# The matmuls for a norm's factors placed behind a stage's first products, in a two-layer model of mixers, attention and experts in fp32

## The chip, the cores and the metric

One core of a Trainium2 chip runs the whole program as one launch. The metric is the device time of an execution in microseconds. Runs of the kernel before agree within 0.1%, so a difference of more than 0.2% is one that its measurement can tell.

## The reference

256 tokens of width 1024 (`h`) go through two layers of a first kind and two of a second kind, all in fp32. Every stage starts with an RMS norm and ends in an addition to `h`:

```python
def rmsnorm(x, g):
    y = x * rsqrt(mean(x * x, axis=-1, keepdims=True) + EPS) * g

# first kind, layers 0 and 1
h = mixer_block(h, ...)            # norm; h @ w_in; retention and gated delta rule; merged @ w_out
u = rmsnorm(h, norm_ffn)
h = h + swiglu(u, ...)             # layer 0: dense, d_ff 2816
h = h + moe(u, ...)                # layer 1: 8 experts of 1408, the best 2 of each token
h = h + sigmoid(rmsnorm(h, norm_ple) @ w_ple_gate) * (p @ w_ple)
# then h = rmsnorm(h, norm_final), and the second kind, layers 0 and 1
u = rmsnorm(h, norm1_g_2)
proj = u @ w_in_2                  # heads of three mixers: attention, an mLSTM, an HGRN
h = h + concat(attention, mlstm, hgrn) @ w_out_2
u = rmsnorm(h, norm2_g_2)
h = h + relu(u @ w_up_2) ** 2 @ w_down_2
```

## The kernel before

`h` lies transposed in SBUF as `hT` (128 channels by 8 blocks `k` by 256 tokens). TensorE runs each fp32 product as three passes: every activation and every weight is split into a rounded part and the remainder (`uhi`, `ulo`, `whi`, `wlo`), and hi·hi, hi·lo and lo·hi are added in PSUM. A product of the stage's input with one weight piece of 256 columns is 48 matmuls of 128x256 (8 blocks, 2 halves, 3 passes).

`piece` (its lines 219, 230 and 231) brings one weight piece of 1 MB in on SyncE's queue, and splits it in two halves: ScalarE rounds (`whi`), VectorE subtracts (`wlo`). `whi` and `wlo` have four half buffers each, so two pieces are split at a time, and the raw pieces have two buffers (in the experts' stage four, `wraw` and `xraw`). Whoever calls `piece` with a pool loads a piece `ahead`, without splitting it.

`norm_T` (L421) makes the stage's input: ScalarE scales `hT` by the norm's gain (`uhi`, L430), VectorE makes `ulo` (L431), both squared on the way into a sum over the 8 blocks (`t`, L402 to L410). The norm's factor per token is left out of `u`; the products are scaled by it afterwards. `by_token` (L418) sums `t` over channels with two matmuls of one column, `rsqrt` (L340 to L351) is a chain of 13 small VectorE operations on 128x2, and `along_tokens` (L444) lays the factor along the free axis: VectorE makes a diagonal `dg` (L453), a matmul of `ones` with it gives `pr` (L454), and ScalarE copies it out as `rsT` (L455). `norm_twice` does it for two norms in a row.

The stages that matter below are `ffn` (layer 0), `moe` (layer 1), `ple`, `_second` (the mixers of the second kind) and `ffn2`. `_second` runs its parts in the order of the list `SECOND`: `hqf` (the first product, in `gemm_b` with `wave`), `mvo`, attention's `aq`, `ak`, `av`, steps of a scan `s`, four steps of attention `a` (each: scores `sm<-ak,aq`, maxima on VectorE, exponentials `pp` on ScalarE, `aa` on VectorE, transposes `sm<-c_base,aa`, a copy `at` on ScalarE, and `sm<-av,at`), `mqk` (the mLSTM's q and k, L1519), `hig`, and the mLSTM's steps `m`. In `mqk` the product in PSUM is multiplied by `rsT` (`cx`, L1527), goes through a convolution of width 4 along the tokens on ScalarE and VectorE (L1532 and L1534), a sigmoid (L1350 to L1352), and becomes `mq` and `mk` (L1538), which the mLSTM multiplies on TensorE (`sm<-mq,mk`, L1731).

`moe` ends with `values_load(mosti)` and `tc.If(n > 128)`: every engine loads the largest number of tokens that an expert has, compares, and takes the branch for a second pass over the experts only where it is above 128 (with these inputs it isn't).

The engines run their own queues in order. What order that is is decided when the program is built: a scheduler of the tile framework orders each engine's instructions by the program's order and by its own estimate of when operands and buffers are free.

Of the kernel before, what the change touches and what calls it, by code (L numbers as in the profile page):

```python
# [150 lines left out]
class Kernel:  # L151
# [102 lines left out]
    def gemm_b(self, x, w, c0, cb, width=256, n=2, tt=False, wave=False):  # L254

        ps = [self.bank("acc") for _ in range(2)]
        if wave:
            wts = [self.piece(w, 0, c0 + i * width) for i in range(n)]
            for t in range(2):
                for j in range(8):  # L260
                    for i in range(n):
                        self.gemm_tok(x, [p[j:j + 1] for p in wts[i]], ps[t][:, i * width:(i + 1) * width], t, k0=j,
                                      start=i == 0 and j == 0, stop=i == n - 1 and j == 7)
                cb(t, ps[t])
            return
# [155 lines left out]
    def norm_T(self, name, rs, xs=None):  # L421
# [18 lines left out]
        r = self.rsqrt(self.by_token(s), 2)  # L440
        rs += [r[:, t:t + 1] for t in range(2)]
        return u
# [15 lines left out]
    def norm_twice(self, n0, n1, rs):  # L458
# [14 lines left out]
        r0 = self.rsqrt(self.by_token(s0), 2)  # L473
        m1 = self.sm.tile([128, 2], F32, name="m01", bufs=1)
        nc.vector.tensor_tensor(m1, r0, r0, OP.mult)
        nc.vector.tensor_tensor(m1, m1, self.by_token(s1), OP.mult)
        r1 = self.rsqrt(m1, 2, name="rt")
        r01 = self.sm.tile([128, 2], F32, name="r01", bufs=1)
        nc.vector.tensor_tensor(r01, r0, r1, OP.mult)
        rs += [r01[:, t:t + 1] for t in range(2)]  # L480
        rT = self.along_tokens([r0[:, t:t + 1] for t in range(2)], name="r0T")
        for k in range(8):
            h = self.hT[:, k, :]
            nc.vector.scalar_tensor_tensor(h, h, g0[:, k:k + 1], rT, op0=OP.mult, op1=OP.mult)
        return u
# [13 lines left out]
    def _mixer(self, l):  # L499
# [5 lines left out]
        if l:  # L505
            rs = []
            u = self.norm_T("norm_mix.1", rs)
            r2 = one([128, 2], "r2")
            rh = [r2[:, t:t + 1] for t in range(2)]
        else:  # L510
            u = self.norm_t(self.rows["norm_mix.0"])
            rs, rh = [1.0] * 2, [0.5] * 2
        convw, gr, gdngn = one([128, 24, 4], "convw"), one([128, 16], "gr"), one([128, 1], "gdngn")
# [114 lines left out]
        def ret_v(i):  # L628
            def cb(t, ps):
                nc.scalar.activation(rv[:, t, i * 512:(i + 1) * 512], ps, AF.Copy, scale=rs[t])  # L630
            self.gemm_b(u, W, 1024 + i * 512, cb, wave=i == 0 and l == 1)
# [194 lines left out]
    def ple(self, l, ple):  # L826
        nc = self.nc
        rs = []
        u = self.norm_T(f"norm_ple.{l}", rs)
        half = self.sm.tile([128, 2], F32, name="half", bufs=1)  # L830
        for t in range(2):
            nc.vector.tensor_scalar(half[:, t:t + 1], rs[t], 0.5, None, op0=OP.mult)
        rT = None
        for i in range(4):
            ps = self.bank("acc")
            self.gemm_a(u, self.piece(f"w_ple_gate.{l}", 0, i * 256), ps, wave=i == 0)
            if rT is None:
                rT = self.along_tokens([half[:, t:t + 1] for t in range(2)])
            two = lambda x: x.rearrange("p (n t) -> p n t", n=2)
            g = self.t2("pg")  # L840
            h = self.hT[:, 2 * i:2 * i + 2, :]
            nc.vector.tensor_tensor(two(g), two(ps), rT[:, None, :].to_broadcast([128, 2, T]), OP.mult)
# [4 lines left out]
    def ffn(self):  # L847
        nc = self.nc
        with self.tc.tile_pool(name="pl0", bufs=1) as self.pp, self.tc.tile_pool(name="ffn", bufs=2) as self.mp:
            rs = []  # L850
            ple, parts = self.ple_table(0)
            u = self.norm_T("norm_ffn.0", rs)
# [4 lines left out]
            down = None  # L857
            for i in range(11):
                ps = []
                for w in ("ffn_w_gate", "ffn_w_up"):  # L860
                    wt = self.piece(w, 0, i * 256)
# [18 lines left out]
                if i < 10:  # L880
                    down = lambda i=i, x=x: self.down_T(x, self.piece("ffn_w_down", 2 * i, 0), acc, i == 0, False)
            self.last_down_T(x, self.piece("ffn_w_down", 20, 0), acc, scale=rsT)
# [1074 lines left out]
```

## Time and profile before

| | us |
|---|---|
| time, median of 3 runs (2192.87 to 2193.52) | 2193.49 |
| the profiled execution, its own time | 2195.91 |
| its span, first to last instruction | 2194.1 |
| TensorE busy in the span | 2066.0 |
| VectorE busy | 1554.9 |
| ScalarE busy | 1212.1 |
| mean granted TensorE clock | 0.963 of full speed |

TensorE has work in 94% of the span; it is idle for 128 us, 10 of them at the start. The granted clock takes two values, full (2.4 GHz) and half (1.2 GHz), and a matmul that runs at half takes about twice as long, while it still counts as busy. So a wait of TensorE may cost more than its own length.

### The profile page before, as it was taken

How to read it: one execution, taken by the hardware profiler on the slowest of the kernel's cores; microseconds unless marked ns; L12 is line 12 of the kernel's file. 1: busy time of each engine (PE TensorE's matmuls, PEld its weight loads, DVE VectorE, ACT ScalarE, POOL GpSimd, SP SyncE). 2: the span in 40 equal slices, each digit the busy share in tenths (PEclk: the TensorE clock that was granted, in tenths of full speed). 3: DMA queues.
4: the chain of work that ended last, by engine and by line, in shares of the span. 5: the costliest groups of instructions: out<-in, count | busy, mean ns of one | idle time of the engine just before them, and what ended most of it. 6: DMA issues, size and time to landing. Idle time of an engine off the chain costs nothing. (4 is left out here: it accounts for less than half of the span.)

```text
span 2194.1 us, 38904 instructions
## 1 busy us (share of the span) xinstructions
PE 2066.0 (94%) x15686; PEld 1977.4 (90%) x15686; DVE 1554.9 (71%) x2837; ACT 1212.1 (55%) x1798; POOL 38.5 (2%) x89
## 2 busy tenths in 40 slices
PE   7999999999899999999999999789789998978999
PEld 7999998999799999988898898788689998878998
DVE  5889486555877986778888888777664557766444
ACT  5554445444564554467777777564445555544554
POOL 0000000000000000000000000020000002000000
PEclk9999999999999999999999999899699999979999
DMA  5454444555445452658989899342135554213553
GB/s 212 164 183 164 126 139 155 193 192 182 142 159 170 173 164 97 223 191 309 330 312 338 302 336 343 123 153 99 56 116 184 185 190 155 97 59 120 188 185 142
DMA packets 81260, 403.03 MB, mean 184 GB/s; under 512 B 25232, under 2 KB 25393, under 8 KB 45361
## 3 DMA queue, kind: packets, MB, share of 16 engines
q1 hardware_dynamic: 61056, 391.66, 50.3%
q10 hardware_dynamic: 17888, 4.39, 1.0%
q0 software_dynamic: 2128, 4.43, 0.7%
q8 instruction: 124, 2.03, 0.4%
q14 instruction: 64, 0.52, 0.1%
HBM read 398.35 MB, written 2.10 MB: 183 GB/s over the span
## 5 line engine op out<-in xcount | busy, mean ns | idle before, releaser
L231 DVE TENSOR_TENSOR wlo<-wraw,whi 128x1024 fp32r<-128x1024 f32 (+3 forms) x644 | 735.6, 1156 | 389.8 <-ACT whi L230 380.4
L230 ACT ACTIVATE whi<-wraw 128x1024 fp32r<-128x1024 f32 (+3 forms) x644 | 634.3, 1005 | 592.2 <-PE acc L251 192.8
L251 PE MATMUL acc<-whi,uhi 128*128 128x256 f32 (+3 forms) x1920 | 554.0, 299 | 22.0 <-DVE hx L1426 12.8
L251 PE MATMUL acc<-whi,ulo 128*128 128x256 f32 (+3 forms) x1920 | 552.5, 298 | 3.8 <-DVE ulo L431 3.8
L251 PE MATMUL acc<-wlo,uhi 128*128 128x256 f32 (+3 forms) x1920 | 546.6, 299 | 8.0 <-DVE wlo L231 7.4
L251 PEld LDWEIGHTS acc<-whi,uhi 128*128 128x128 f32 x1920 | 361.5, 193 | 27.9 <-issue 13.2
L251 PEld LDWEIGHTS acc<-wlo,uhi 128*128 128x128 f32 x1920 | 359.2, 193 | 15.5 <-DVE wlo L231 14.6
L251 PEld LDWEIGHTS acc<-whi,ulo 128*128 128x128 f32 x1920 | 362.0, 193 | 5.0 <-DVE ulo L431 4.2
L293 PE MATMUL sm<-uhi,whi 128*128 128x256 f32 x864 | 244.3, 283 | 0.0
L293 PE MATMUL sm<-ulo,whi 128*128 128x256 f32 x864 | 243.6, 282 | 0.0
L293 PE MATMUL sm<-uhi,wlo 128*128 128x256 f32 x864 | 243.5, 282 | 0.0
L293 PE MATMUL acc<-uhi,whi 128*128 128x256 f32 x704 | 199.3, 284 | 10.2 <-ACT whi L230 10.2
L293 PE MATMUL acc<-uhi,wlo 128*128 128x256 f32 x704 | 199.6, 284 | 1.7 <-DVE wlo L231 1.7
L293 PE MATMUL acc<-ulo,whi 128*128 128x256 f32 x704 | 199.3, 284 | 1.3 <-DVE ulo L317 1.3
L231 DVE TENSOR_TENSOR wlo<-xraw,whi 128x704 fp32r<-128x704 f32 (+1 forms) x176 | 166.0, 978 | 34.1 <-ACT whi L230 31.5
L230 ACT ACTIVATE whi<-xraw 128x704 fp32r<-128x704 f32 (+1 forms) x176 | 144.4, 860 | 50.6 <-PE acc L251 15.6
L293 PEld LDWEIGHTS sm<-uhi,whi 128*128 128x128 f32 x864 | 165.6, 192 | 0.6
L293 PEld LDWEIGHTS sm<-ulo,whi 128*128 128x128 f32 x864 | 165.0, 191 | 0.6
L293 PEld LDWEIGHTS sm<-uhi,wlo 128*128 128x128 f32 x864 | 164.9, 191 | 0.0
L293 PEld LDWEIGHTS acc<-uhi,whi 128*128 128x128 f32 x704 | 134.0, 191 | 10.8 <-ACT whi L230 10.4
L293 PEld LDWEIGHTS acc<-uhi,wlo 128*128 128x128 f32 x704 | 134.0, 190 | 2.2 <-DVE wlo L231 2.1
L293 PEld LDWEIGHTS acc<-ulo,whi 128*128 128x128 f32 x704 | 133.9, 190 | 1.9 <-DVE ulo L317 1.7
(650 smaller groups left out, 3355.9 us busy)
## 6 DMA issues: line engine op xcount, KB each, us to landing
wraw<-in_w_in SPq DMA_DIRECT2D x80, 1024.0 KB, 4.8
wraw<-in_w_up SPq DMA_DIRECT2D x32, 1024.0 KB, 4.8
wraw<-in_w_down SPq DMA_DIRECT2D x32, 1024.0 KB, 4.8
xraw<-in_exp_w_down SPq DMA_DIRECT2D x24, 1024.0 KB, 7.3
xraw<-in_exp_w_gate SPq DMA_DIRECT2D x32, 704.0 KB, 5.3
xraw<-in_exp_w_up SPq DMA_DIRECT2D x32, 704.0 KB, 5.6
wraw<-in_exp_w_gate SPq DMA_DIRECT2D x32, 704.0 KB, 5.4
wraw<-in_exp_w_up SPq DMA_DIRECT2D x32, 704.0 KB, 5.8
```

The source lines that it names most:

```text
L230: nc.scalar.activation(hi[:, :mm], raw[:, s], AF.Copy)
L231: nc.vector.tensor_tensor(lo[:, :mm], raw[:, s], hi[:, :mm], OP.subtract)
L251: nc.tensor.matmul(o, a[:, k0 + j, ts], b[j], start=start and i == 0 and j == 0, stop=stop and i == 2 and j == n - 1)
L293: self.nc.tensor.matmul(ps[:, n * 256:(n + 1) * 256], a[j][:, n * 128:(n + 1) * 128], b[:, j, :], start=(n, j, i) == (0, 0, 0), stop=(n, j ...
```

## The change

Nothing is computed otherwise. In text order:

- `norm_T` and `norm_twice` return the input and a function `fin`, which holds `by_token`, the rsqrt chain (and in `norm_twice` the scaling of `hT`). The caller runs `fin`, and `along_tokens` behind it, after the stage's first products.
- The first weight piece of a stage is asked for ahead of `norm_T`, so that its split stands ahead of the norm's tiles on ScalarE and VectorE.
- `gemm_b` with `wave` goes over blocks 0 to 5 for both token halves and then over 6 and 7, and calls `mid` (there `fin`) ahead of its callbacks.
- In `_second`, `rsT` is made in this `mid`, and no longer in `mqk`.
- `ple` makes two of its four products ahead of `fin`.
- The last step of `ffn` and of the first `ffn2` makes its up products ahead of the previous step's down products.
- `moe` runs the branch ahead of the main pass over the experts, and loads one experts' piece `ahead` instead of one of `w_ple_gate.1`.

```diff
     def gemm_b(self, x, w, c0, cb, width=256, n=2, tt=False, wave=None, mid=None):
         ps = [self.bank("acc") for _ in range(2)]
         if wave:
-            wts = [self.piece(w, 0, c0 + i * width) for i in range(n)]
+            for js in (range(6), range(6, 8)):
+                for t in range(2):
+                    for j in js:
+                        for i in range(n):
+                            self.gemm_tok(x, [p[j:j + 1] for p in wave[i]], ps[t][:, i * width:(i + 1) * width], t, k0=j,
+                                          start=i == 0 and j == 0, stop=i == n - 1 and j == 7)
+            mid()
             for t in range(2):
-                for j in range(8):
...
                 cb(t, ps[t])
             return
...
     def norm_T(self, name, rs, xs=None):
...
-        r = self.rsqrt(self.by_token(s), 2)
-        rs += [r[:, t:t + 1] for t in range(2)]
-        return u
+        def fin():
+            r = self.rsqrt(self.by_token(s), 2)
+            rs.extend(r[:, t:t + 1] for t in range(2))
+
+        return u, fin
...
     def ple(self, l, ple):
...
+        wt = w(0)
+        u, fin = self.norm_T(f"norm_ple.{l}", rs)
...
+        self.gemm_a(u, wt, ps[0], wave=True)
+        self.gemm_a(u, w(1), ps[1])
+        fin()
...
+        rT = self.along_tokens([half[:, t:t + 1] for t in range(2)])
...
     # ffn
-            u = self.norm_T("norm_ffn.0", rs)
+            first = self.piece("ffn_w_gate", 0, 0)
+            u, fin = self.norm_T("norm_ffn.0", rs)
             for f in parts:
                 f()
...
                     self.gemm_a(u, wt, ps[-1], wave=i == 0 and len(ps) == 1)
-                    if rsT is None:
-                        rsT = self.along_tokens(rs)
...
+                if i == 0:
+                    fin()
+                    rsT = self.along_tokens(rs)
...
     # moe
-        self.experts(uk, pos, ghl, rhl, 0)
...
-        self.piece("w_ple_gate.1", 0, 0, self.pp)
+        self.piece("exp_w_gate.0", 0, 0, self.pp)
         n = nc.values_load(mosti[0:1, 0:1], min_val=0, max_val=256)
+        ahead, self.ahead = self.ahead, {}
         with self.tc.If(n > 128):
             self.experts(uk, pos, ghl, rhl, 1)
+        self.ahead = ahead
+        self.experts(uk, pos, ghl, rhl, 0)
...
     # _second
+        wave = [self.piece(W, 0, 2568 + i * 256) for i in range(2)]
...
-            self.gemm_b(u, W, 2568, cb, wave=True)
+            def mid():
+                fin()
+                rsT.append(self.along_tokens(rs))
+
+            self.gemm_b(u, W, 2568, cb, wave=wave, mid=mid)
...
         def g_mqk():
-            rsT.append(self.along_tokens(rs))
             for i, nm in enumerate(("q", "k")):
...
     # ffn2
+            first = self.piece(f"w_up_2.{l}", 0, 0)
+            u, fin = self.norm_T(f"norm2_g_2.{l}", rs)
...
-                if i == 3 and not l:
-                    rsT = self.along_tokens(rs2)
...
+                if i == 3:
+                    fin()
+                    for t in range(2):
+                        nc.vector.tensor_tensor(rs2[t], rs[t], rs[t], OP.mult)
+                    if not l:
+                        rsT = self.along_tokens(rs2)
```

How the built programs stand, at three places. First TensorE's queue in the mixers of layer 0, where the last steps of attention (`av`, `at`, `aa`), the factor's matmuls (`dg`) and the last products of `hig` meet the first of the mLSTM; before:

```order
L1809 MATMUL sm<-av,at 128x128
L1810 MATMUL sm<-av,at 128x128
L1811 MATMUL sm<-av,at 128x128
L454 MATMUL sm<-dg,ones 128x128 x2
L251 MATMUL acc<-wlo,uhi 128x256
L251 MATMUL acc<-whi,uhi 128x256
L251 MATMUL acc<-whi,ulo 128x256
L251 MATMUL acc<-wlo,uhi 128x256
L1731 MATMUL sm<-mq,mk 128x256
L1732 MATMUL sm<-mq,mk 128x128
L1805 MATMUL sm<-c_base,aa 128x128 x3
L1809 MATMUL sm<-av,at 128x128
```

The same place of the changed kernel:

```order
L1836 MATMUL sm<-av,at 128x128
L1837 MATMUL sm<-av,at 128x128
L1838 MATMUL sm<-av,at 128x128
L1758 MATMUL sm<-mq,mk 128x256
L1759 MATMUL sm<-mq,mk 128x128
L251 MATMUL acc<-wlo,uhi 128x256
L251 MATMUL acc<-whi,uhi 128x256
L251 MATMUL acc<-whi,ulo 128x256
L251 MATMUL acc<-wlo,uhi 128x256
L1832 MATMUL sm<-c_base,aa 128x128 x3
```

The factor's two matmuls are gone from here (they stand some 580 rows ahead, among the first products), and the mLSTM's first scores stand ahead of the last four products.

Second VectorE's queue at the end of the same stage, around the mLSTM's k (`mk`) and attention's last step (maxima `amx` and `anb`, weights `aw` and `aa`); the changed kernel:

```order
L1700 COPY_PREDICATED hS<-c_second,sm 128x128x2
L1813 TENSOR_REDUCE amx<-sm 128x3
L1565 TENSOR_TENSOR mk<-cv,sg 128x512
L1814 TENSOR_TENSOR amx<-amx 128x1
L1813 TENSOR_REDUCE amx<-sm 128x3
L1816 SCALAR_TENSOR_TENSOR anb<-amx,ars 128x2
L1814 TENSOR_TENSOR amx<-amx 128x1
L1816 SCALAR_TENSOR_TENSOR anb<-amx,ars 128x2
L1574 TENSOR_SCALAR hx<-acc,r_20855 128x256
L1823 RECIPROCAL aw<-osum 128x4
L1824 COPY oss<-aw 128x2
```

`mk` stands inside attention's last step, and the convolutions that it needs stand ahead of that; in the kernel before `cx`, both convolutions and `mk` stand behind the whole step.

Third TensorE's queue in `ffn` of layer 0, behind the 96 matmuls of the first gate and up products; the changed kernel:

```order
L296 MATMUL sm<-uhi,wlo 128x256
L421 MATMUL sm<-ones,t_4178 128x1 x2
L460 MATMUL sm<-dg,ones 128x128
L296 MATMUL sm<-uhi,whi 128x256
L296 MATMUL sm<-ulo,whi 128x256
```

`by_token`'s two matmuls (`ones,t`) now stand right ahead of the diagonal's (`dg,ones`), which needs the rsqrt chain between them; before, 96 rows stood between the two.

## Rows read from the trace of the kernel before

**Rows 1.** The page: busy us by engine, and DMA busy by slice.

```profile
PE 2066.0 (94%) x15686; PEld 1977.4 (90%) x15686; DVE 1554.9 (71%) x2837; ACT 1212.1 (55%) x1798; POOL 38.5 (2%) x89
...
DMA  5454444555445452658989899342135554213553
```

**Rows 2.** TensorE's timeline (start, duration, instruction, idle before and its releaser).

```profile
1551.01 0.61 PE L454 MATMUL sm<-dg,ones 128*128 128x128 f32 x4
...
1566.06 1.19 PE L1731 MATMUL sm<-mq,mk 64*128 64x256 f32 x2 [13.97 <-DVE mk L1538]
...
1592.11 0.77 PE L768 MATMUL acc<-uhi,whi 128*128 128x256 f32 x2
```

**Rows 3.** The timeline of VectorE, the first operation on `mqk`'s products.

```profile
1552.07 0.69 DVE L1527 TENSOR_TENSOR cx<-acc,rsT 128x512 f32<-128x512 f32 x1 [0.22 <-ACT rsT L455]
```

**Rows 4.** The timeline of TensorE, the last of the 96 products of `mqk`.

```profile
1530.69 0.28 PE L293 MATMUL acc<-uhi,wlo 128*128 128x256 f32 x1
```

**Rows 5.** Windows: us, busy of PE, PEld, DVE, ACT, POOL; clock, DMA share, GB/s.

```profile
1500.00:1505.00 5.00, 5.00 (x20) 3.69 (x19) 1.53 (x7) 1.98 (x5) 0.00 (x0) 0.50 0.01 3
1522.00:1528.00 6.00, 6.00 (x56) 5.01 (x55) 4.34 (x14) 0.23 (x2) 0.00 (x0) 1.00 0.00 0
1566.00:1592.10 26.10, 25.46 (x113) 22.94 (x114) 14.78 (x55) 6.16 (x14) 0.00 (x0) 0.50 0.00 1
1955.00:1967.00 12.00, 11.26 (x60) 10.31 (x60) 10.86 (x47) 3.68 (x8) 0.00 (x0) 0.52 0.00 1
1631.00:1638.30 7.30, 7.30 (x64) 7.30 (x64) 3.31 (x4) 3.88 (x6) 0.00 (x0) 1.00 0.30 93
```

**Rows 6.** The timeline of TensorE at the same place of layer 1.

```profile
1942.44 0.28 PE L251 MATMUL acc<-wlo,uhi 128*128 128x256 f32 x1
1954.90 1.23 PE L1731 MATMUL sm<-mq,mk 64*128 64x256 f32 x4 [12.18 <-DVE mk L1538]
```

**Rows 7.** The timeline of ScalarE, then (last row) of VectorE.

```profile
1547.46 0.49 ACT L1807 ACTIVATE at<-sm 128x384 f32<-128x384 f32 x1
1549.53 1.06 ACT L230 ACTIVATE whi<-wraw 128x1024 fp32r<-128x1024 f32 x1 [0.88 <-PE acc L251]
...
1571.10 1.15 ACT L1822 ACTIVATE sq<-mix 128x512 f32<-128x512 f32 x2
...
1578.27 1.29 DVE L1830 TENSOR_TENSOR mix<-mix,or 128x512 f32<-128x512 f32 x2
```

**Rows 8.** The timeline of TensorE at the start of both `ffn2`.

```profile
1624.72 0.56 PE L418 MATMUL sm<-ones,t 128*128 128x1 f32 x2 [7.89 <-DVE t L410]
...
1638.20 0.28 PE L293 MATMUL sm<-uhi,wlo 128*128 128x256 f32 x1
...
2004.02 0.98 PE L418 MATMUL sm<-ones,t 128*128 128x1 f32 x4 [7.87 <-DVE t L410]
...
2018.92 0.28 PE L293 MATMUL sm<-uhi,wlo 128*128 128x256 f32 x1
```

**Rows 9.** The timeline of TensorE in `ffn`, then of VectorE in `ffn2`.

```profile
359.89 1.01 PE L418 MATMUL sm<-ones,t 128*128 128x1 f32 x4 [4.57 <-DVE t L410]
...
2005.04 0.16 DVE L340 TENSOR_SCALAR rq<-sm 128x2 f32<-128x2 f32 x1 [1.17 <-PE sm L418]
...
2007.41 0.23 DVE L1841 TENSOR_TENSOR rs<-rq 128x1 f32<-128x1 f32 x2
```

**Rows 10.** The branch (L988, ns min/median/max); the page's DMA issues; ScalarE's timeline.

```profile
L988 PEldq COMPARE_BRANCH  x1: 3646/3646/3646, 1386.3 to 1386.3; - x1
...
xraw<-in_exp_w_gate SPq DMA_DIRECT2D x32, 704.0 KB, 5.3
...
1391.31 0.63 ACT L402 ACTIVATE t<-hT 128x512 f32<-128x512 f32 x1 [7.30 <-DVEq L988]
```

**Rows 11.** TensorE's timeline in `ple` and `_second`, both of layer 1.

```profile
1397.17 0.58 PE L293 MATMUL acc<-uhi,whi 128*128 128x256 f32 x1 [10.22 <-ACT whi L230]
...
1835.88 0.56 PE L251 MATMUL acc<-whi,uhi 128*128 128x260 f32 x1 [5.34 <-DVE hx L1426]
```

More of the change, by code (lines that the diff above doesn't have):

```diff
@@ L252, in gemm_tok, with gemm_b @@
                                  stop=stop and i == 2 and j == n - 1)
[L254 removed]
+    def gemm_b(self, x, w, c0, cb, width=256, n=2, tt=False, wave=None, mid=None):
         ps = [self.bank("acc") for _ in range(2)]
         if wave:
[L258 removed]
+            for js in (range(6), range(6, 8)):
[5 more added lines that the diff above has]
+            mid()
             for t in range(2):
[L260 to L263 removed]
                 cb(t, ps[t])
@@ L472, in norm_twice, with fin @@
             step1(p)
[L473 to L485, printed above, removed]
+        def fin():
+            r0 = self.rsqrt(self.by_token(s0), 2)
+            m1 = self.sm.tile([128, 2], F32, name="m01", bufs=1)
+            nc.vector.tensor_tensor(m1, r0, r0, OP.mult)
+            nc.vector.tensor_tensor(m1, m1, self.by_token(s1), OP.mult)
+            r1 = self.rsqrt(m1, 2, name="rt")
+            r01 = self.sm.tile([128, 2], F32, name="r01", bufs=1)
+            nc.vector.tensor_tensor(r01, r0, r1, OP.mult)
+            rs.extend(r01[:, t:t + 1] for t in range(2))
+            rT = self.along_tokens([r0[:, t:t + 1] for t in range(2)], name="r0T")
+            for k in range(8):
+                h = self.hT[:, k, :]
+                nc.vector.scalar_tensor_tensor(h, h, g0[:, k:k + 1], rT, op0=OP.mult, op1=OP.mult)
+        return u, fin
     def mixer(self, l):
@@ L506, in _mixer @@
             rs = []
-            u = self.norm_T("norm_mix.1", rs)
+            wave = [self.piece(W, 0, 1024 + i * 256) for i in range(2)]
+            u, fin = self.norm_T("norm_mix.1", rs)
             r2 = one([128, 2], "r2")
@@ L630, in cb @@
                 nc.scalar.activation(rv[:, t, i * 512:(i + 1) * 512], ps, AF.Copy, scale=rs[t])
-            self.gemm_b(u, W, 1024 + i * 512, cb, wave=i == 0 and l == 1)
+            self.gemm_b(u, W, 1024 + i * 512, cb, wave=wave if i == 0 else None, mid=fin)
         def ret(h):
@@ L856, in ffn @@
             acc = [self.bank("acc") for _ in range(4)]
-            down = None
+            down, last = None, []
             for i in range(11):
@@ L881, in ffn @@
                     down = lambda i=i, x=x: self.down_T(x, self.piece("ffn_w_down", 2 * i, 0), acc, i == 0, False)
+                    if i == 9:
+                        last, down = [down], None
+            last[0]()
             self.last_down_T(x, self.piece("ffn_w_down", 20, 0), acc, scale=rsT)
@@ L927, in _moe @@
         nc.vector.tensor_copy(lT, pl[0:8, :T])
+        parts[2]()
+        fin()
         for t in range(2):
@@ L1879, in ffn2 @@
                     down = lambda i=i, x=x: self.down_T(x, self.piece(f"w_down_2.{l}", 2 * i, 0), acc, i == 0, False)
+                    if i == 14:
+                        last, down = [down], None
             if l:
@@ L1885, in ffn2 @@
             else:
+                last[0]()
                 self.last_down_T(x, self.piece(f"w_down_2.{l}", 30, 0), acc, scale=rsT)
```

36 lines of the change are left out of this document (16 added, 20 removed).

## The prediction, made before the run

> **What bounds the kernel now.** I read the page first: TensorE is busy in 94% of the span, VectorE in 71%, ScalarE in 55% [rows 1]. So time is won where TensorE waits, and where it works at half clock. I then listed every TensorE row with idle time in front of it (the timeline), and set windows around them for the granted clock. The idle rows are few and long, and they have two causes. Five stand where a stage begins: the sum of squares `t`, or what is computed from it, or a weight split is last [rows 8, 9, 11]. The two longest stand inside the mixers of the second kind, and their releaser is `mk`, the mLSTM's k [rows 2, 6]. The reader should see in the windows what follows a long wait: from 1566 to 1592 us TensorE has matmuls all the time, at a clock of 0.50 [rows 5]. Such a stretch counts as busy and costs twice its work.
>
> **The long waits for `mk`.** The 96 products that `mk` and `mq` come from are done at 1530.7 us [rows 4], but the first operation on them, `cx`, starts at 1552.07 and waited last for ScalarE's `rsT` [rows 3]. The two matmuls that `rsT` comes from ran at 1551.01 [rows 2], because `mqk` asks for them in text order behind most of attention. So the whole chain of two convolutions and two sigmoids, 1552.07 to 1566, lies behind the last work that could have covered it. The change makes `rsT` in `mid`, some 580 rows of TensorE earlier. The changed order shows what the scheduler makes of it: `cx` and the convolutions now stand between attention's steps, and `mk` stands inside the last step.
>
> *Term D, layer 0.* Removed: the idle 13.97 us [rows 2]. What comes in its place: ScalarE's `at` now stands behind a split `whi` whose buffer becomes free with the last products, and a copy: 1.06 + 0.49 + 0.49 us (the copy taken like `at`) [rows 7], of which TensorE's three transposes cover half a us, so 1.5 us of new wait. The convolutions' VectorE work, now between attention's maxima and weights, delays its steps: not in the trace, bounded by 0 and 3, taken as 1.5. If the clock stays at half in the tail all the same, D is 13.97 - 1.5 - 1.5 = 11.0. If it stays full, the 25.46 us of work at 0.50 [rows 5] shrink by 12.7, but then attention's own chain becomes late: from its squares to its scaled result takes 1571.10 to 1579.56 [rows 7], and TensorE, twice as fast, is there some 2.5 us ahead. D is then 11.0 + 12.7 - 2.5 = 21.2. Which of the two? A stretch of small matmuls without idle stands at full clock from 1522 to 1528, another at half from 1500 to 1505 [rows 5]; so both occur, and I take the middle, **16**.
>
> The Trainium skill (TensorE: Matmul & The Clock Gate, "HAM oscillation — how this bites in real kernels") puts the fall of the clock down to idle gaps. By that rule the tail would run at full clock and D would be 21.2; the stretch from 1500 to 1505 is TensorE at half with no idle, so the trace does not bear the rule out alone.
>
> *Term G, layer 1.* The same place: idle 12.18 [rows 6], and 11.26 us of work at 0.52 [rows 5]. Half clock kept: 12.18 - 1.5 - 1 = 9.7. Full: + 5.6 - 2 = 13.3. Taken **11.5**.
>
> **The starts of both `ffn2`.** Now TensorE waits until `t` is summed, does `by_token`, and only then the first up product; from the last product of the stage before (1624.72 - 7.89 = 1616.83) to the end of the first two up products (1638.48) are 21.65 us; in layer 1 from 1996.15 to 2019.20, 23.05 us [rows 8]. The 96 matmuls of two products need 0.114 us each at full clock (7.30 us for 64 [rows 5]), so 10.9. In the changed order the first piece's split stands ahead of the norm's tiles, `by_token` stands some 250 rows later, and its chain and diagonal are well apart there, so nothing waits for them. What is left is that the blocks of `u` arrive one pair after another. If that costs nothing, the stages win 21.65 - 10.9 = 10.7 and 23.05 - 10.9 = 12.1. If it keeps the clock at half through one of the two products, 5.5 less: 5.2 and 6.6. Middles: *term E* **8** and *term H* **9.3**.
>
> **The start of `ffn`.** *Term A.* The idle 4.57 [rows 9] in front goes. But `by_token` and `dg` are now neighbours on TensorE, and the rsqrt chain must run between them: 1.17 us to its first operation, 2.6 to its end (2005.04 to 2007.64 [rows 9]), and the diagonal behind it. So about 4.3 us of wait come back some 15 us later, with the same drop of the clock. Bounds +2.8 (the clock doesn't drop at one of the two) and -2.9 (it drops at both); I take **-1**. Behind them on TensorE's queue are the third gate and up products, which have nothing else to wait for.
>
> **`ple` and the mixers of layer 1 of the first kind.** *Term B.* The edits there replace short waits by short waits (VectorE has the second piece's split ahead of three of four `ulo` pairs). Bounds 0 and -2.8, one clock drop; taken **-1**.
>
> **The experts.** *Term C.* The branch is moved, not removed. At the end of the experts it holds ScalarE for 7.30 us [rows 10], and TensorE sits idle 10.22 us [rows 11]. There it goes, and TensorE can win up to 8. But `norm_twice` behind `ple` needs `ple`'s result, and its factor is now made behind two products instead of one: most of it is waited for again, and I keep 2.2. At the front, every engine now reads the register and fetches behind the branch: 3.65 us on TensorE [rows 10], in front of the gather. And SyncE, which in the order before asks for five pieces of weights ahead of the register's load, now asks for all but one behind the branch: 5.3 us until one lands [rows 10] and some 2 to split it, against about 5 of gather and first piece. Together -6 (-4 to -9). C is **-3.8**, bounds -9 and +4.
>
> The Trainium skill prices a compare-and-branch at about 108 ns (Advanced Engine Details and Errata, "Control Flow Timing"), and says elsewhere that a branch breaks the sequential prefetch (Runtime: NRT & Kernel Launch, "Instruction fetch mechanics"). By the first alone the entry would cost 2.4 instead of 6 and C would be -0.2; the trace's 3646 ns on TensorE's queue speaks for the second.
>
> **The start of the mixers in layer 1 of the second kind.** *Term F.* The idle 5.34 [rows 11] has the releaser `hx`, which stands behind two weight splits on VectorE. That order is unchanged, and two diagonals now stand ahead of `hx`: **-0.7**, bounds -1.5 and +0.5.
>
> **The sum.** -1 - 1 - 3.8 + 16 + 8 - 0.7 + 11.5 + 9.3 = 38.3 us. The profiled execution would go from 2195.9 to 2157.6, and the median of the runs, which is 2.4 below it, to **2155**. All lower bounds together give a gain of 16 (2177), all upper ones of 65 (2129).
>
> **Rivals.**
> 1. *The tail keeps half clock and attention pays for the convolutions.* TensorE does not wait for `mk` any more, but for `aa` and `at`, whose VectorE and ScalarE work now queues behind `cv` operations; the order speaks for it (six of them stand inside one step), the trace's idle VectorE there against it. D and G at their lower bounds less 3 us each, entry at -9: 38.3 - 8 - 4.8 - 5.2 = 20; time 2173.
> 2. *The clock holds through both tails.* D 21.2, G 13.3, E and H at their upper bounds: 38.3 + 5.2 + 1.8 + 2.7 + 2.8 = 51; time 2143.
> 3. *The change doesn't do what it says:* the `mk` wait is replaced by an equally long one, since the mLSTM's steps also need attention's last step out of the way. Then D and G fall to about nothing, and 11 are left: 2183. If the starts of `ffn2` give nothing either, it is the same as before.
> 4. *Slower: the experts' weights are late throughout.* The experts' stage runs 176 pieces (8 experts of 22) with DMA busy nine tenths in its slices [rows 1]; it has lost its head start of four pieces. If from then on each piece came 0.22 us later than now, 38 us would be gone, and the kernel is slower from there on. Against it: the ring of four buffers, not the head start, sets the pace of the issues, and a late start is paid once.
>
> **Chances.** The forecast (2148 to 2167) 0.55; rival 1 (2167 to 2180) 0.2; rival 2 (under 2148) 0.16; rival 3 0.06, of which half within 0.2% (4.4 us); rival 4 with 0.03, slower. A difference below 0.2% is one that this measurement can't tell from none. Faster by more than that: 0.94, the same 0.03, slower 0.03. The range from 2140 to 2176 leaves out a tenth at either end.
>
> **What would show it.** In the changed profile: no long idle before the first `sm<-mq,mk`, and `cx` of layer 0 within a few us of its products (D, G); the windows over the small matmuls behind it tell the clock; the first up product of both `ffn2` within 1 us of the last product before it (E, H); a new idle of about 4 us before `sm<-dg,ones` in `ffn` (A); 4 us of idle in front of the experts' gather and waits for `exp_w` (C). I am wrong if attention's `aa` or `at` releases TensorE after more than 3 us at several steps, or if the mean clock stays at 0.963.

## The result and the profile after

The changed kernel takes 2159.2 us (median of 4 runs, 2153.8 to 2161.2), the kernel before beside it 2193.2 (2192.8 to 2193.5). The ratio is 0.9841, 95% interval 0.9823 to 0.9859: 34.0 us faster. The forecast was 2155, its range 2140 to 2176. The profiled execution took 2161.2 us.

The page after, busy times:

```profile
span 2159.4 us, 38877 instructions
PE 2078.5 (96%) x15686; PEld 1988.7 (92%) x15686; DVE 1546.7 (72%) x2837; ACT 1209.9 (56%) x1799; POOL 35.6 (2%) x89
```

From the end of the first mixer to the last down product, 1834.8 us became 1798.0. I cut that into windows of 2.5 us and summed two things over them: what TensorE was not busy went from 108.3 to 60.4 us, and the half-clock loss (one minus the granted clock, times the busy time) from 53.2 to 62.6. So the gain is idle time, and none of it is clock. That is the main thing to take from the two traces.

TensorE's rows after, at the places that the prediction speaks of (start, duration, then the idle time in front and its releaser):

```profile
373.62 0.50 PE L421 MATMUL sm<-ones,t 128*128 128x1 f32 x4
378.52 0.46 PE L460 MATMUL sm<-dg,ones 128*128 128x128 f32 x2 [4.40 <-DVE dg L459]
...
948.43 0.48 PE L1085 MATMUL sm<-c_base,P 128*128 128x128 f32 x1 [3.72 <-ACTq L1009]
...
1384.60 0.50 PE L296 MATMUL acc<-uhi,whi 128*128 128x256 f32 x2 [0.86 <-ACT uhi L433]
1387.24 0.58 PE L296 MATMUL acc<-ulo,whi 128*128 128x256 f32 x1 [2.14 <-DVE ulo L434]
...
1551.49 0.70 PE L1758 MATMUL sm<-mq,mk 64*128 64x256 f32 x2
1554.84 0.49 PE L1836 MATMUL sm<-av,at 128*128 128x128 f32 x2 [1.45 <-ACT at L1834]
...
1601.68 0.28 PE L779 MATMUL acc<-uhi,wlo 128*128 128x256 f32 x1
1601.80 0.28 PE L296 MATMUL sm<-uhi,whi 128*128 128x256 f32 x1
...
1814.15 1.22 PE L460 MATMUL sm<-dg,ones 128*128 128x128 f32 x4 [7.25 <-DVE dg L459]
...
1919.80 0.74 PE L1832 MATMUL sm<-c_base,aa 128*128 128x128 f32 x3 [1.11 <-DVE aa L1827]
1922.45 0.80 PE L1836 MATMUL sm<-av,at 128*128 128x128 f32 x2 [1.91 <-ACT at L1834]
1924.03 1.23 PE L1758 MATMUL sm<-mq,mk 64*128 64x256 f32 x4
1926.42 0.67 PE L1766 MATMUL sm<-mv,wm 128*128 128x66 f32 x2 [0.73 <-DVE wm L1760]
```

- The `sm<-mq,mk` rows carry no idle: the 13.97 and 12.18 us of [rows 2, 6] are gone. Small waits for attention's `at` and `aa` stand near them, none above 1.91 us.
- `ffn2`'s first up product follows `w_out`'s last product at once (1601.68, 1601.80), where there were 7.89 and 7.87 us [rows 8].
- In `ffn` the 4.57 us of [rows 9] turned into 4.40 in front of the diagonal.
- The experts' gather waits 3.72 us behind the branch. `ple`'s first product, behind the experts, waits 0.86 and 2.14 instead of 10.22 [rows 11].
- The 5.34 us of [rows 11] at the start of layer 1's mixers became 7.25.

VectorE after: the first operation on the products, at 1552.07 in [rows 3], is 39.7 us sooner (7.8 of it from the stages ahead), and `mk` is there before it is wanted.

```profile
1512.41 0.69 DVE L1554 TENSOR_TENSOR cx<-acc,rsT 128x512 f32<-128x512 f32 x1 [0.82 <-PE acc L296]
1543.05 0.68 DVE L1565 TENSOR_TENSOR mk<-cv,sg 128x512 f32<-128x512 f32 x1
```

Windows after, to set against [rows 5] (length, busy times, then the granted clock as a share of full speed):

```profile
1542.00:1549.00 7.00, 7.00 (x31) 5.79 (x30) 2.62 (x8) 2.66 (x10) 0.00 (x0) 0.57 0.36 143
1556.00:1582.00 26.00, 26.00 (x132) 24.72 (x131) 18.03 (x85) 6.01 (x14) 0.00 (x0) 0.54 0.11 41
1921.00:1948.00 27.00, 24.82 (x120) 23.44 (x121) 15.79 (x57) 7.68 (x18) 0.00 (x0) 0.52 0.10 40
```

TensorE is busy through both tails, and both run at the lower level (1.2 GHz) without the long wait that stood ahead of them before. In layer 1 the half-clock stretch is longer than it was.

### The profile page after: what moved, and what is told of

Its sections match the earlier page's. It is cut to its first block, busy times and chain, and to the rows that moved or that the text cites. A ratio compares the mean times of both kernels' runs of the same rounds, so it can differ in the third digit from the quotient of the medians.

```text
span 2159.4 us, 38877 instructions
## 1 busy us (share of the span) xinstructions
PE 2078.5 (96%) x15686; PEld 1988.7 (92%) x15686; DVE 1546.7 (72%) x2837; ACT 1209.9 (56%) x1799; POOL 35.6 (2%) x89
## 4 chain that ended last, share of the span: by engine, by line
PE 41%; DMA 6%; DVE 4%; ACT 2%; issue 1%; POOL 0%; ACTq 0%; DVEq 0%
PE acc L251 17%; PE sm L296 8%; PE acc L779 6%; DVE wlo L231 3%; PE acc L296 2%; DMA xraw<-in_exp_w_gate 2%; ACT whi L230 2%; PE sm L1694 1%; DMA xraw<-in_exp_w_down 1%; DMA xraw<-in_exp_w_up 1%; DMA wraw<-in_exp_w_up 1%; PE sm L1094 1%; PE sm L1811 1%; PE sm L1065 0%; PE sm L312 0%
```

## The experiments

**How they are read.** Besides the times I cut each trace into stages at TensorE rows that all kernels have: the end of the mixer ahead of `ffn`, `ffn`'s last down product, the first router product, the `sel` product, the first gather product `sm<-P,ukh`, the last `sm<-PT`, the last product of 260 columns (`mvo`), `w_out`'s last, `ffn2`'s last, and the same in layer 1. The half-clock loss of a stage is the sum above over that stage. Where a new order moves products across a mark, the gain of one stage is the loss of its neighbour. The expectations of experiments 1 and 4 read a gain of 12.1 us for D and 3 for E from the trace after; by the marks used here the same two traces give 7.0 and 8.4, with nearly the same sum.

Beside the experiments the kernel before ran from 2184.8 to 2200.9 us, so its runs agree within 0.7% and not within the 0.1% that was given ahead; the differences below are judged by the intervals of their ratios.

**1. `rsT` early, alone** (in the kernel before).

```
             self.gemm_b(u, W, 2568, cb, wave=True)
+            rsT.append(self.along_tokens(rs))
...
         def g_mqk():
-            rsT.append(self.along_tokens(rs))
```

> The kernel before, with one edit: along_tokens(rs) for mlstm's convolutions stands right behind the first wave of products (in g_hqf) and no longer in g_mqk; nothing else of the change. Theory A (read from the trace after: D gained 12.1 and G 4.1, because the wait for mk goes but the small matmuls behind it still run at half clock): 16 us less than before, 2177; no idle of more than 3 us in front of sm<-mq,mk in either layer, and the granted clock 0.50 in both tails. Theory B (the forecast's middles, 16 and 11.5): 27.5 less, 2165.7, and full clock in a part of the tails. Rival (the early factor was not what the waits hung on): within 4 us of before, and the idles of 13.97 and 12.18 us stay.

2175.5 us, ratio 0.9916 (0.9893 to 0.9939), 18.8 less than before on its chip. Theory A. From `mvo` to `w_out` layer 0 took 135.1 us instead of 142.9, layer 1 141.8 instead of 151.4. Windows of its two tails, at half clock:

```profile
1562.00:1572.00 10.00, 10.00 (x49) 8.93 (x47) 8.13 (x41) 1.25 (x3) 0.00 (x0) 0.50 0.00 0
1940.00:1950.00 10.00, 8.69 (x48) 8.18 (x47) 7.16 (x36) 1.20 (x3) 0.00 (x0) 0.53 0.00 1
```

**2. `rsT` late again** (in the changed kernel).

```
-            def mid():
-                fin()
-                rsT.append(self.along_tokens(rs))
-
-            self.gemm_b(u, W, 2568, cb, wave=wave, mid=mid)
+            self.gemm_b(u, W, 2568, cb, wave=wave, mid=fin)
...
         def g_mqk():
+            rsT.append(self.along_tokens(rs))
```

> The changed kernel, with along_tokens(rs) for the convolutions back in g_mqk; all else stays. Theory A: the idles of 12 to 14 us in front of sm<-mq,mk come back in both layers, and it costs what D and G gained in the trace, 16 us: 2175. Theory B (the forecast): 27.5, 2186.7. Rival (the gain of the mixers comes from other edits): within 4 us of the changed kernel.

2175.8 us, ratio 0.992 (0.9897 to 0.9943), 17 above the changed kernel by the ratios. Theory A, from the other side, and TensorE's rows (the timeline) have the old waits back:

```profile
1561.87 1.19 PE L1755 MATMUL sm<-mq,mk 64*128 64x256 f32 x2 [12.03 <-DVE mk L1562]
1939.80 1.23 PE L1755 MATMUL sm<-mq,mk 64*128 64x256 f32 x4 [12.18 <-DVE mk L1562]
```

**3. The branch behind the main pass again.**

```
+        self.experts(uk, pos, ghl, rhl, 0)
         most, mosti = ...
-        self.piece("exp_w_gate.0", 0, 0, self.pp)
+        self.piece("w_ple_gate.1", 0, 0, self.pp)
...
-        self.ahead = ahead
-        self.experts(uk, pos, ghl, rhl, 0)
```

> The changed kernel, with the experts' branch back behind their main pass, and the first piece of w_ple_gate asked for ahead of it, as before. The trace after says: the entry cost 5.4 us, the exit gained about 5 by the end of the next mixer's mvo products, and the main pass between them was 6.2 us shorter. Theory A (the shorter main pass belongs to the branch's place, by the phase in which the weights' buffers go round): all of it goes back, 5.9 us slower than the changed kernel, 2165, and the main pass takes 422 us again. Theory B (the main pass is shorter for another reason): 0.3 faster, 2159, with the main pass at 416. Theory C (the forecast: a loss of 3.8): 2155.4.

2155.6 us, ratio 0.9826 (0.9801 to 0.9851). Theory C by the median; the interval alone doesn't exclude the changed kernel's 0.9842. The stages decide. From `sel` to the gather: 3.1 to 3.6 us in the four traces with the branch behind, 7.5 to 8.2 in the ten with it ahead. From the gather to the last `sm<-PT`: 433.2 to 439.3, mean 436.6, against 435.2 to 447.4, mean 441.3. So the main pass that had looked shorter in the first trace after was chance: its 435.2 is the shortest of the ten.

**4. `ffn2`'s norm in front again.**

```
-            first = self.piece(f"w_up_2.{l}", 0, 0)
+            first = None
             u, fin = self.norm_T(f"norm2_g_2.{l}", rs)
+            fin()
...
-                if i == 3:
-                    fin()
...
```

> The changed kernel, with the two ffn2 stages' norm as before: by_token and its factor in front of the first up product, whose weight split stands behind the norm's tiles. Theory A (the trace after: E gained 3, H 10.6): 13.6 us slower than the changed kernel, 2172.8, of it about 3 in layer 0. Theory B (the forecast: 8 and 9.3): 17.3 slower, 2176.5, with 8 of it in layer 0. Rival (the early products only wait elsewhere): within 4 us.

2169.3 us, ratio 0.9885 (0.9864 to 0.9906), some 10 above the changed kernel. The stages gave back more: `ffn2` 191.2 instead of 182.7 in layer 0 (8.5, Theory B's 8), 192.7 instead of 183.8 in layer 1 (8.9). TensorE's rows have the idles of before:

```profile
1604.89 0.98 PE L421 MATMUL sm<-ones,t 128*128 128x1 f32 x4 [7.61 <-DVE t L413]
1974.12 0.98 PE L421 MATMUL sm<-ones,t 128*128 128x1 f32 x4 [7.87 <-DVE t L413]
```

But the start of layer 1's mixers behind layer 0's `ffn2` took 34.0 us here, 39.9 to 40.2 with `ffn2` as changed. Of these 5.9 us, 0.8 are eight small matmuls (`sm<-c_base,sg` and `sm<-c_base,hx`) that stand behind the `mvo` mark here and ahead of it in the changed kernel. So some 5 of the 8.5 us that the early start wins in layer 0 went again at the next stage; experiment 10 takes up the wait there.

**5. The changed kernel once more**, no edit.

> The changed kernel once more, unedited, on the chip of the three experiments sent with it. By the first measurement 0.984 of before, some 2159 us. It also gives a second trace of the same instructions. Theory A (the granted clock in the mixers' tails differs from execution to execution): the stretch from the last attention product to the last hv,hS product, which lost 12.7 us to half clock in layer 0 and 11.4 in layer 1, loses another amount this time, by 3 us or more in one of the layers. Theory B (the clock follows from the instructions alone): the same two amounts within 1.5 us.

2159.5 us, ratio 0.9842 (0.9827 to 0.9857). Theory A: the stretch (from the last `sm<-ak,aq` to the last `sm<-hv,hS`) lost 5.1 us instead of 12.7 in layer 0; in layer 1 it was the same, 11.5 and 11.4. In layer 0's tail the clock was down for one short stretch only (windows):

```profile
1556.00:1566.00 10.00, 8.35 (x60) 7.06 (x58) 8.95 (x22) 7.91 (x20) 0.00 (x0) 1.00 0.31 106
1566.00:1576.00 10.00, 9.96 (x50) 9.48 (x50) 8.22 (x41) 1.76 (x3) 0.00 (x0) 0.53 0.00 0
```

So one trace doesn't say what the clock costs in a tail. From here on I use all traces that have the same code in a stage.

**6. Diagonals apart from `by_token`.**

```
                     self.gemm_a(u, wt, ps[-1], wave=i == 0 and len(ps) == 1)
+                    if i == 0 and len(ps) == 1:
+                        fin()
...
                 if i == 0:
-                    fin()
                     rsT = self.along_tokens(rs)
...
-            self.gemm_b(u, W, 2568, cb, wave=wave, mid=mid)
+            self.gemm_b(u, W, 2568, cb, wave=wave, mid=fin)
...                                         # in g_mvo, behind its products
+            if self.late:
+                self.late()                 # norm_twice's r0T and its use
+            rsT.append(self.along_tokens(rs))
```

> The changed kernel with the diagonals moved apart from by_token: in ffn, fin stands behind the first gate product and along_tokens behind the first up product; in the mixers of the second kind along_tokens (and norm_twice's r0T) stands behind mvo's products. Theory A (TensorE waits there only because the diagonal stands at the head of its queue): the idles of 4.4 us in ffn, 4.0 in layer 0 and 7.25 in layer 1 in front of sm<-dg,ones go, with part of the half clock behind them, and 12 us are won, 2147. Theory B (behind the diagonal the next thing is just as late, since hx and the copies that free the accumulators need the same factors): the idles in the mixers come back at 5 to 6 us in front of acc<-whi,uhi of mvo, only ffn's goes, and 5 us are won, 2154.

2143.2 us, ratio 0.9757 (0.9727 to 0.9787), 16 less than the changed kernel beside it (runs from 2126.6 to 2151.2). Theory A in `ffn` (191.4 instead of 197.5, no idle left) and at layer 0's mixers (last `sm<-PT` to `mvo`: 73.3 instead of 82.5, of which eight small `sm<-dg,ones`, now behind the mark, are 1 to 2 us). Theory B in layer 1: 39.7 instead of 39.9, and the wait has only passed on (TensorE's rows):

```profile
1443.92 0.36 PE L251 MATMUL acc<-whi,uhi 128*128 128x260 f32 x1 [1.71 <-DVE hx L1456]
...
1795.97 0.56 PE L251 MATMUL acc<-whi,uhi 128*128 128x260 f32 x1 [7.89 <-ACT mv L1498]
```

**7. Wide products among the tail's small ones.**

```
             nc.vector.scalar_tensor_tensor(wm[:, h, :], ps[:, 0:384], ...)
+            self.wide(ps, 8)
...                                         # hgrn_scores, behind copy_predicated
+                if b < 2:
+                    self.wide(ps, 4)
```

> The changed kernel with 48 products of 128x256 more in each mixer of the second kind, whose results nothing reads: 8 behind each of the mLSTM's four score steps, and 4 behind each half of the last two steps of hgrn's scores, into banks that are free there. So they stand between the small matmuls of the tail. They cost 5.5 us a layer at full clock, 11 at half. Theory A (the clock falls since the tail has too little wide work, not by its short waits): the granted clock stays near 1.00 from the last attention product to the last hv,hS product, the 10 to 13 us lost there to half clock go down to 3 or less, and each layer wins some 4 us net: 2151. Theory B (the clock falls by the waits that begin the tail, and nothing in the tail brings it back): 5 to 11 us slower in each layer, 2170 to 2181, and the clock still 0.50.

2157.3 us, ratio 0.9843 (0.9809 to 0.9876): no different, with runs from 2149.8 to 2171.1. The one trace looks like Theory A in layer 0 and like Theory B in layer 1 (windows, the first of layer 0, the others of layer 1):

```profile
1556.00:1572.00 16.00, 16.00 (x130) 14.93 (x130) 12.16 (x50) 3.72 (x8) 0.00 (x0) 1.00 0.14 58
1905.00:1913.00 8.00, 5.10 (x44) 4.64 (x42) 5.87 (x11) 7.22 (x19) 0.00 (x0) 1.00 0.32 112
1914.00:1940.00 26.00, 25.56 (x107) 23.37 (x108) 10.71 (x46) 3.04 (x6) 0.00 (x0) 0.50 0.07 31
```

In layer 1 TensorE was busy 5.10 of 8 us ahead of the tail, and then the clock stayed down for 26 us of nearly unbroken work, 45 wide products in it.

**8. The waits at the tail's beginning filled** (layer 1; the scheduler puts all 26 in one row).

```
+                if po is not None:          # attention's last step
+                    wide(10)
                 pt = self.bank("sm")
...
+                if po is not None:
+                    wide(16)
```

> The changed kernel with 26 products of 128x256 more in layer 1's mixer of the second kind, whose results nothing reads, in one row ahead of attention's last three transposes; so they fill the waits of 1.11, 1.91 and 0.73 us with which the tail begins. They cost 3.0 us at full clock. Nothing is added further back in the tail. Theory A (the clock falls by the waits at the tail's beginning): it stays at 1.00 behind them, the 18 us that the three stretches of layer 1's mixer lose to half clock in the changed kernel go down to 7 or less, and 11 us are won, 2148. Theory B (the small matmuls behind are enough to let it fall): it is 0.50 in the tail all the same, for 8 us or more, and the time is within 3 us of the changed kernel, 2156 to 2162.

2157.0 us, ratio 0.9832 (0.9806 to 0.9858): Theory B, by the time and by the clock, which was at 0.50 for 12 us. It held at 1.00 through the filled stretch and fell behind a new wait (1.61 us for `wm`; one of 2.21 for `or` follows). Its windows, and TensorE's rows with the new waits:

```profile
1917.00:1935.00 18.00, 17.63 (x141) 15.62 (x139) 12.97 (x33) 11.95 (x31) 0.00 (x0) 1.00 0.17 59
1937.00:1949.00 12.00, 9.79 (x47) 9.54 (x47) 5.17 (x30) 2.55 (x5) 0.00 (x0) 0.50 0.01 2
```

```profile
1936.24 0.64 PE L1766 MATMUL sm<-mv,wm 128*128 128x66 f32 x2 [1.61 <-DVE wm L1760]
1941.23 1.94 PE L312 MATMUL sm<-c_base,mix 128*128 128x128 f32 x8 [2.21 <-DVE or L1867]
```

The half-clock loss of layer 1's mixer was 10.8 us here, and 18.1 and 18.0 in the two traces of the changed kernel. But two other traces without a filler in this stage lost 8.5 (experiment 3) and 13.6 (experiment 4), so this one trace does not show that the filling did it.

**9. A third raw buffer, by every second piece.**

```
-        with self.tc.tile_pool(name=f"sec{l}", bufs=2) as self.mp:
+        with self.tc.tile_pool(name=f"sec{l}", bufs=2) as self.mp, self.tc.tile_pool(name=f"sraw{l}", bufs=1) as self.raw:
...
```

> The changed kernel with a third raw buffer for weights in the mixers of the second kind (ropa and ropb have one buffer instead of two to make room; all of their operations are VectorE's, in order). Theory A (the rsqrt chain is late at the start of layer 1's mixers because a weight split stands ahead of it on VectorE, and that split waits for a transfer that was asked for at 1801.49 and landed at 1809.3): with one more buffer the transfer is asked for earlier, the idle of 7.25 us in front of sm<-dg,ones falls to 3 or less, and 4 us or more are won, 2155. Theory B (the chain is late by its own length and the splits' work): the idle stays above 5 us, and the time within 2 us of the changed kernel.

2154.5 us, ratio 0.9807 (0.9785 to 0.9829), but the idle is still there, and so is the wait for the transfer: the piece took the buffer of the piece two before it (rows of ScalarE and TensorE). The experiment missed its target, and whatever its median gains is not at that place; its interval overlaps that of the changed kernel.

```profile
1807.08 1.06 ACT L230 ACTIVATE whi<-xraw 128x1024 fp32r<-128x1024 f32 x1 [6.74 <-DMA xraw<-in_w_in]
1812.13 1.22 PE L460 MATMUL sm<-dg,ones 128*128 128x128 f32 x4 [7.19 <-DVE dg L459]
```

**10. A third raw buffer, by every third piece.**

```
-            elif self.raw is None or self.turn == 0:
+            elif self.raw is None or (self.turn == 0 if self.cyc is None else self.cyc % 3 < 2):
...
```

> The changed kernel with a third raw buffer in the mixers of the second kind again, this time taken in turn by every third piece (in a_raw every second piece took it, so each waited for the split of the one two pieces before, as ever). Theory A (layer 1's rsqrt chain stands on VectorE behind a weight split that waits for a late transfer): the fifth piece's transfer is now asked for right behind the second piece's split, ahead of the norm's tiles; the split no longer waits for it, the idle in front of sm<-dg,ones in layer 1 falls from 7.25 to 3.5 or less, and 4 us are won there. Theory B (the chain is late by its own length): the idle stays above 5.5 us and nothing is won.

2146.2 us, ratio 0.9781 (0.9759 to 0.9802). First the changed kernel's rows at that place (SyncE's queue, ScalarE, VectorE):

```profile
1801.49 0.33 SPq L219 DMA_DIRECT2D wraw<-in_w_in  x1
1809.30 2.00 ACT L230 ACTIVATE whi<-wraw 128x1024 fp32r<-128x1024 f32 x2 [6.99 <-DMA wraw<-in_w_in]
1807.18 0.16 DVE L354 SCALAR_TENSOR_TENSOR rq<-rq,rq 128x2 f32<-128x2 f32 x1
1810.39 1.23 DVE L231 TENSOR_TENSOR wlo<-wraw,whi 128x1024 fp32r<-128x1024 f32 x1 [3.04 <-ACT whi L230]
1811.53 0.15 DVE L352 TENSOR_TENSOR rq<-rq 128x2 f32<-128x2 f32 x1
1811.60 1.22 DVE L231 TENSOR_TENSOR wlo<-wraw,whi 128x1024 fp32r<-128x1024 f32 x1
...
1813.60 0.15 DVE L354 SCALAR_TENSOR_TENSOR rq<-rq,rq 128x2 f32<-128x2 f32 x1
```

The factor's chain `rq` stands still from 1807.34 to 1811.53, since `wlo` is next on VectorE, and `wlo` waits through `whi` for a transfer asked for at 1801.49. With the third buffer in turn (SyncE's queue, ScalarE, TensorE):

```profile
1787.27 0.33 SPq L223 DMA_DIRECT2D wraw<-in_w_in  x1
1802.75 1.06 ACT L234 ACTIVATE whi<-wraw 128x1024 fp32r<-128x1024 f32 x1 [3.08 <-PE acc L255]
1808.63 1.23 PE L464 MATMUL sm<-dg,ones 128*128 128x128 f32 x4 [4.36 <-DVE dg L463]
```

The transfer is asked for 5.3 us behind layer 0's last down product (1781.99) instead of 16.9 (1784.62), the split waits for TensorE instead, the idle is 4.36, and the stage takes 36.2 us instead of 39.9. Of the 3.7 us, 0.8 are again the eight small matmuls at the mark, so 2.9 are won, as much as the idle fell. That is Theory A in kind, short of its sizes (3.5 of idle, 4 us won). Layer 0's start gained as well (76.8 instead of 82.5), which I had not expected.

**11. Late diagonals and the branch behind.** Edits 3 and 6 together.

> The two edits that were faster than the changed kernel together: the diagonals moved apart from by_token (a_dg_late, 0.9757 of before) and the experts' branch back behind their main pass (a_if_behind, 0.9826, where the changed kernel has 0.984). Theory A (they lie in different stages and add up): 3 to 4 us less than a_dg_late, 0.974 of before, 2139. Theory B (the exit's wait for the branch, 7 us in a_if_behind, takes back what the later diagonals win at the start of the mixer behind it): no better than a_dg_late, 2143 to 2147.

2150.3 us, ratio 0.9786 (0.9762 to 0.981). Theory B, and some 3 us above its range: the exit waits 7.24 us as in experiment 3, the stage from the last `sm<-PT` to `mvo` is back at 84.6, and a new wait of 4.88 us for `aa` stands in layer 0.

**12. Late diagonals and the third buffer.** Edits 6 and 10 together.

> The changed kernel with the two edits together that have done best: the diagonals moved apart from by_token (a_dg_late, 0.9757 of before) and the third raw buffer taken in turn in the mixers of the second kind (a_raw3, 0.9781). The branch stays ahead of the main pass. Theory A (they add up where they meet different waits): ffn keeps the 6.1 us of a_dg_late, the start of layer 0's mixer keeps the larger of the two gains there (9 and 6 us), and the start of layer 1's mixer takes 36 us or less instead of 40, since there the diagonal's move alone only passed the wait on to mv: 5 us less than a_dg_late, 0.9735 of before, 2138. Theory B (at the start of layer 1's mixer the factors stay late for hx and mv whatever the buffers): that stretch stays at 39 us or more and the time at that of a_dg_late, 0.9757, 2143.

2137.2 us (2134.0 to 2151.0), ratio 0.9760 (0.9733 to 0.9787). The stages nearly follow Theory A: `ffn` 191.4, layer 0's start 71.3, layer 1's 36.8 (it had 36). The ratio can't be told from that of a_dg_late, which is Theory B's. So both beat the two kernels of the case, the changed one by some 16 to 19 us, and which of them is better stays open.

## Why the prediction was right, and where its steps were not

The time came out 4 us above the forecast, and that is partly luck: D, F and G won 11.7 us less than forecast, A 5.3 more. Gains in us, from the mean over all traces that have the old or the new code in a stage and no other edit there (their number in brackets; in D and G the kernel of experiment 1 counts as new, that of experiment 2 as old):

| term | forecast (bounds) | old | new | gain |
|---|---|---|---|---|
| A, `ffn` | -1 (-2.9 to 2.8) | 202.1 [2] | 197.8 [9] | 4.3 |
| B, `ple0` and mixers through the router to `sel` | -1 (-2.8 to 0) | 386.2 [2] | 386.3 [10] | -0.1 |
| C, entry + main pass + exit | -3.8 (-9 to 4) | 527.6 | 531.6 | -4.0 |
| D, `mvo` to `w_out`, layer 0 | 16 (11 to 21.2) | 141.4 [2] | 130.8 [6] | 10.6 |
| E, `ffn2(0)` | 8 (5.2 to 10.7) | 191.2 [3] | 182.7 [11] | 8.5 |
| F, start of layer 1 | -0.7 (-1.5 to 0.5) | 36.7 [2] | 40.0 [4] | -3.3 |
| G, `mvo` to `w_out`, layer 1 | 11.5 (9.7 to 13.3) | 151.5 [2] | 143.7 [5] | 7.8 |
| H, `ffn2(1)` | 9.3 (6.6 to 12.1) | 193.5 [3] | 183.8 [11] | 9.7 |

The gains sum to 33.5. C is the gather, the main pass and the stretch to `mvo`: 3.3 + 436.6 + 87.7 [4, 4, 3] against 7.7 + 441.3 + 82.6 [10, 10, 4].

- **D and G, the clock: the step that failed.** "I take the middle" between a clock kept at half and one kept full. The means of the half-clock loss show no gain: layer 0 lost 17.3 and 15.3 us with the wait, and 10.2 to 22.2, mean 15.6, without; layer 1 12.3 twice, and 8.5 to 18.1, mean 13.6, without. The waits themselves went as said (14.6 us of idle in layer 0's tail became 1.4 to 3.8, 13.3 in layer 1's 3.8 to 5.4), and what came in their place was `at` and `aa`, as the term had it. So D is near its lower bound, the one for half clock kept. G is 2 below it: the new waits are some 3.4 us instead of 2.5, since `wm` waits too, and the mean half-clock loss is 1.3 larger. That is rival 1's clock, with part of its price. Experiments 1 and 2 show that the place of `rsT` is what removes the `mk` wait.
- **A: mis-sized by 5.3, since an edit had no price.** The 4.40 us of idle came where it was forecast. But the same diff puts `ffn`'s last-but-one down product behind the last gate and up products, and I gave that nothing. At the end of the stage the old traces wait for that product's input `hhi`, the new ones don't (TensorE's rows before):

```profile
550.62 0.74 PE L768 MATMUL acc<-hhi,whi 128*128 128x256 f32 x4 [2.18 <-ACT hhi L877]
```

  The idle of the stage went from 7.1 to 4.4 us, and its half-clock loss from 3.1 to 1.7, where the term had no gain. No run moves that product back alone. Experiment 6 confirms the other half: with the diagonal apart the stage is 6.1 shorter.
- **B** is right, near its upper bound. At the first router product itself the trace seems to show a loss of 2.6 us ahead and a gain of 2.9 behind. But 24 of the products `sm<-pThi,whi` and their like stand right ahead of that router product in the changed kernel, and 5 before; the 19 that changed sides are 2.2 us at 0.114 us each.
- **C** is right in sum, with both parts larger: the entry costs 4.4 at the gather and 4.7 in the main pass (whose traces differ by 12, and which has 2.0 more half-clock loss and 1.4 more idle in the mean), where I had 6 (4 to 9); the stretch at the exit wins 5.1, where I had 2.2.
- **E and H** are right in the number, 8.5 and 9.7 for 8 and 9.3, but not for the reason of their middles. The clock does not fall there at all: the half-clock loss of both stages is 0.0 in all eleven traces, so by the term's own reasoning the upper bounds 10.7 and 12.1 were due. In layer 0 of the trace after, the first two products take 12.0 us instead of 10.9, and the rest of the stage is 1.2 longer, with `by_token` in it.
- **F failed.** "That order is unchanged" is not so. Before, one step of the factor's chain stands behind the first half of the fifth piece's split and `hx` right behind the second (SyncE's queue, VectorE):

```profile
1826.61 0.33 SPq L219 DMA_DIRECT2D wraw<-in_w_in  x1
1832.64 1.23 DVE L231 TENSOR_TENSOR wlo<-wraw,whi 128x1024 fp32r<-128x1024 f32 x1 [0.91 <-ACT whi L230]
1833.78 0.15 DVE L351 SCALAR_TENSOR_TENSOR rq<-rq,rq 128x2 f32<-128x2 f32 x1
1833.85 1.22 DVE L231 TENSOR_TENSOR wlo<-wraw,whi 128x1024 fp32r<-128x1024 f32 x1
1834.99 0.74 DVE L1426 TENSOR_SCALAR hx<-acc,rq 128x512 f32<-128x512 f32 x1
```

  After, six steps stand behind the first half, five of them behind the second (1812.74 to 1813.75; experiment 10 shows the last), and then the diagonals. The split itself starts 24.7 us behind layer 0's last down product instead of 23.6: its transfer is asked for sooner (16.9 us instead of 18.6), but takes 7.7 us to land instead of 4.8. In the means the idle of the stage grew only from 9.4 to 9.8 us, the half-clock loss from 2.3 to 4.0, and 0.8 us are the eight small matmuls at the mark. Experiment 10 names the wait. Why the transfer took longer stays open, and so does the part of `ffn2`: with the old one the stage took 34.0 in experiment 4 and 36.7 before.
- **Rivals.** 2 (the clock holds) and 3 (an equal wait for `mk`) did not happen. Rival 4's pieces were not late throughout: 4.7 us over the main pass instead of 38.
- **The signs.** I had written that I am wrong if the mean clock stays at 0.963. It is 0.964 in this trace and 0.967 to 0.969 in the other three runs of the first four. So the sign all but came, and it was right about D and G, whose middles counted on clock that was not won. The time is right all the same, since the gain was idle time. The other sign, waits of more than 3 us for `aa` or `at`, did not come in this trace (1.91 at most).

## What to carry to other kernels

Price every edit of a diff, also those that only look like a consequence: the stage with the moved down product made up part of what the clock did not give. Before a gain is put down to a stage, see that both traces have the same products between its marks: 19 that had changed sides looked like a gain of 2.9 us at the router. Before a term of a few us is read from two traces, look at a stage that both share: here the experts' main pass differed by 12 us with the same code, and layer 0's mixer by 10 between two traces of one kernel. Where a chain of small operations sets a stage's start, see what stands ahead of it on its engine and which transfer that waits for; diagonals placed some products later, with or without a third buffer, gave another 16 to 19 us.

## What was unexpected of the hardware

- The granted clock can differ between executions of the same instructions: in layer 0's tail the changed kernel was at 0.54 for 26 us in one, and down for some 10 us in the other.
- Once down, it stayed down for 26 us of work with 0.44 us of idle, 45 wide products of 128x256 among it (experiment 7); in another kernel, that of experiment 3, it was back in layer 1's tail after some 7 us of small matmuls (windows):

```profile
1925.00:1931.00 6.00, 6.00 (x37) 5.76 (x37) 5.50 (x32) 0.39 (x1) 0.00 (x0) 0.50 0.00 1
1932.00:1945.00 13.00, 12.70 (x111) 12.51 (x110) 9.17 (x43) 4.67 (x7) 0.00 (x0) 1.00 0.01 1
```

And it fell where TensorE had no idle time at all (1542 to 1549 in the trace after, 7.00 of 7.00 us busy, 0.57); no row of that stage ahead of it, from 1466 on, has even 0.2 us of idle in front.

The Trainium skill (TensorE: Matmul & The Clock Gate, "HAM oscillation — how this bites in real kernels") blames idle gaps. Experiment 8's one trace fits that in layer 1's tail, where the clock held through the filled 18 us and fell behind a wait; the fall from 1542 on has no gap ahead of it and does not fit. What brings it back after 7 us in one execution and after 27 in another is not settled by these runs.
